# PEER layer in two passes: a larger top-k budget per expert row in the first, leftover blocks spread through the second

## The chip, the cores and the metric

The kernel runs on one core of a Trainium2 chip, as one launch. The metric is the device time of one execution in microseconds (us). The kernel before has a median of 4171.94 us over three runs.

## What is computed

The reference is a float32 model on 256 tokens of width 1024 and 256 context tokens: two blocks of one kind, then two of another. Only the first kind's PEER layer matters here. It is a feed-forward layer that picks experts by product keys:

```python
def chunk(hc):                                   # 128 tokens
    q = (hc @ w_query).reshape(128, 8, 2, 64)
    s = einsum('chpd,hpnd->chpn', q, sub_keys)   # scores of 2 x 128 keys per head
    s_top, i_top = lax.top_k(s, 16)
    cand = s_top[:, :, 0, :, None] + s_top[:, :, 1, None, :]
    best, pos = lax.top_k(cand.reshape(128, 8, 256), 16)
    eid = ...                                    # expert = 128 * i + j, of 16384
    gate = softmax(best)
    act = gelu(einsum('chkd,cd->chk', u_tab[eid], hc)) * gate
    return einsum('chk,chkd->cd', act, v_tab[eid])
```

In the first of the two layers it runs over 512 tokens (x and context), in the second over 256.

## The kernel before

The kernel does not gather experts for most tokens. It computes the activation of all 16384 experts for all tokens, multiplies by a gate matrix that is zero except at each token's picks, and multiplies by the whole V table. All products are made three times in a split of float32 into a high and a low half (`mm3`: high x high, high x low, low x high, lines 371 to 373). Each weight piece is 128 x 1024 (512 KB): it is loaded on the SP queue (`raw`, line 344), rounded to its high half `wh` on ScalarE (line 339), and its low half `wl` is the difference, on VectorE, or on GpSimd for every `share`-th piece (line 340). There are four `raw` buffers and two each of `wh` and `wl`.

`peer(0)` treats the 512 tokens in four groups of 128. The first group (`g0` = 128) is done by rows: its top-k gives expert numbers, `rows_up` gathers one U row per token and step with GpSimd and makes the dot product on VectorE (line 1159), and `rows_down` gathers V rows and accumulates on VectorE (line 1178). The other 384 tokens go through the whole table, in two passes:

- **The U pass.** An expert row is 128 experts: 24 matmuls of 384 columns into one bank, and a gelu on ScalarE (line 1238). A block, `ublock`, is four rows, and there are 32 blocks. After each row the loop takes steps of the top-k generator, `budget` units' worth (each step yields its cost), at a raised priority. It also takes `rate["up"]` steps of `rows_up` once the first group's top-k is ready. The top-k is scores on TensorE, searches on VectorE (lines 1006 to 1061), and for the three table groups a one-hot expansion (lines 1101 to 1133): VectorE writes `oa` and `ob`, TensorE multiplies them, ScalarE copies, GpSimd adds into `stg`, and the gate matrix is stored to `gd` in DRAM. A finished block's activations `a4` are stored to `ad` in DRAM on ScalarE's queue. The pass ends after the block in which the top-k runs out; `nb` is the number of blocks done. A tail follows, in which what remains of the top-k is worked off.
- **The V pass.** The 32 blocks are taken two at a time (`deep` = 2). `prep(b)` loads the block's gates and activations, multiplies them (line 1297) and splits them. For a block that the U pass left over (`b >= nb`) it computes the four expert rows on the spot, with all low halves on VectorE (`share` = 0). Then, for each of eight output slices `d`, 24 matmuls go into one bank and VectorE adds the result to `xt` (line 1304). After each slice come `rate["down"]` steps of `rows_down`. Blocks are prepared up to two ahead. There are two `a4` buffers.

The code is traced in program order, and a planner with its own costs then sets each engine's order from priorities and from what is ready; the engines run their lists strictly in that order. The order of the V blocks is one leftover block first, then all the others by number:

```python
order = list(range(32))
if nb < 32:
    order = [nb] + order[:nb] + order[nb + 1 :]
```

`peer(1)` uses the same function with 256 tokens, no rows and a budget of 2.0. It leaves four blocks to its V pass, one at the start and three at the end.

Of the kernel before, what the change touches and what calls it, by code (L numbers as in the profile page):

```python
# [233 lines left out]
class Kernel:  # L234
# [748 lines left out]
    ratio2 = (1.0, 1.3)  # L983
    on_pool = 6
    pool_x = (0, 0, 0, 0, 0, 0, 0, 0)
    rate = {("gate", 0): (10, 0, 2), ("gate", 1): (4, 0, 2), ("u", 0): 0, ("u", 1): 0, ("v", 0): 0, ("v", 1): 1.25, "mix": (5, 1.3), "up": 1.22, "down": 1.15, "ffn": 1.4, "out": 1, "att": (0.4, 0.4), "norm": ((4,4), (2,2), (4,4), (4,4))}


    def topk(self, l, tt, tp, qT, gd, keep):
# [191 lines left out]
    def peer(self, l, budget):  # L1181
# [3 lines left out]
        g0 = self.rows_at(l)  # L1185
# [4 lines left out]
        with ExitStack() as es:  # L1190
# [7 lines left out]
            up = None  # L1198
# [6 lines left out]
            with self.pool(f"tp{l}") as tp:  # L1205
# [43 lines left out]
                nb = owed = 0  # L1249
                while not done and nb < 32:  # L1250
                    for a4 in ublock(4 * nb):
# [9 lines left out]
                        if g0 and "ready" in dst:  # L1261
                            if up is None:
                                up = self.rows_up(tp, dst, x)
# [17 lines left out]
            with self.pool(f"vp{l}") as vp:  # L1281
# [54 lines left out]
                if g0:  # L1336
                    acc = self.t(vp, [P, D], "racc")
                    down = self.rows_down(vp, dst, acc)
                    self.steps = 0
                order = list(range(32))  # L1340
                if nb < 32:
                    order = [nb] + order[:nb] + order[nb + 1 :]
                todo = [prep(b) for b in order[: wb - deep]]
                bias = self.bias_load(vp) if l == 0 else None
# [312 lines left out]
    def run(self):  # L1657
        self.setup()

        self.filler = self.adaln(self.mod1[0], self.v("b_mod0"))  # L1660
        for s in (1, 0):
            cols = slice(s * T, s * T + T)
            self.nc.sync.dma_start(self.xt[:, :, cols], self.A["xt"][:, :, cols])
            for d in range(8):
                self.track(d, s)
        self.mixer(0)
        self.need(60)
        if self.stop == "mix0":
            return self.dump()

        self.peer(0, 3.1)
        if self.stop == "peer0":
            return self.dump()
        self.mixer(1)
        if self.stop == "mix1":
            return self.dump()
        self.peer(1, 2.0)
        if self.stop == "peer1":
            return self.dump()
        with self.more_weights(2, 0), self.pool("bp") as bp:  # L1680
            self.bp = bp
            with self.banks(sc=2):
                self.enter(0, 0)
            self.sums_begin(bp, 2, (2,), self.sums_of("adat", 72, self.mod2[1], "ada_b1", lambda m: (2,)))
            self.ffn(0, 0, (0, 1))
            self.mixer2(0, (0, 2))
            self.ffn(0, 1, (1, 0))
            self.ffn(1, 0, (1, 1))
            self.mixer2(1, (1, 2))
            self.ffn(1, 1, None)  # L1690
# [20 lines left out]
```

## Time and profile before

| | |
|---|---|
| median of 3 runs | 4171.94 us (4168.49 to 4172.41) |
| the profiled execution | 4176.94 us, span 4175.2 us |
| TensorE busy, mean granted clock | 92% of the span, 0.945 |
| VectorE busy | 77% |
| ScalarE, GpSimd busy | 43%, 23% |
| DMA | 944.96 MB, mean 226 GB/s |

The time is that of the whole execution, and the span runs from the first to the last instruction in the trace. Busy is the share in which an engine executes. A granted clock of 1.00 is TensorE's full speed. PEld is TensorE's weight load, which overlaps its matmuls.

### The profile page before, as it was taken

Reading aid. Unit: us, or ns where it says so; the run is one execution under the profiler, and the core shown is the slowest. Engines: PE = TensorE matmul, PEld = TensorE weight load, DVE = VectorE, ACT = ScalarE, POOL = GpSimd, SP = SyncE. Lnnn points to the kernel's source line nnn. Section 1 sums busy time; section 2 is a strip of 40 time slices with the busy share of each in tenths; the row PEclk is TensorE's granted clock in tenths of the full one; section 3 lists DMA queues with packets and bytes.
Section 4 is the critical chain, followed back from the end, with each engine's and each line's share of the span. In section 5 each row is a group of like instructions: output and inputs, shape, how many; then the busy total and the mean of one; then the engine's idle time right before and its main releaser. Section 6 shows DMA issues by size and latency. Waiting matters only on the chain.

```text
span 4175.2 us, 69284 instructions
## 1 busy us (share of the span) xinstructions
PE 3820.4 (92%) x25443; PEld 3562.4 (85%) x25443; DVE 3235.8 (77%) x7950; ACT 1794.7 (43%) x2986; POOL 968.9 (23%) x803
## 2 busy tenths in 40 slices
PE   7889898978897699999899999999989989999898
PEld 5568798978786599998689999999989879998798
DVE  4768778988987699996768997898868778656664
ACT  3342333433444233333344656444444554444543
POOL 0100014654634233440302848000000010100100
PEclk9999999999896799999899999999999989999899
DMA  5436548888756999984235767999869439554244
GB/s 181 157 103 216 184 156 292 290 287 279 251 191 176 254 348 345 340 324 140 98 117 186 251 234 254 378 363 341 310 232 315 155 104 320 159 184 146 95 162 142
DMA packets 331123, 944.96 MB, mean 226 GB/s; under 512 B 30832, under 2 KB 118512, under 8 KB 330784
## 3 DMA queue, kind: packets, MB, share of 16 engines
q1 hardware_dynamic: 201776, 722.15, 49.8%
q0 software_dynamic: 38272, 137.38, 10.3%
q10 hardware_dynamic: 90736, 81.01, 5.9%
q8 instruction: 201, 3.29, 0.3%
q14 instruction: 138, 1.13, 0.1%
HBM read 855.23 MB, written 85.19 MB: 225 GB/s over the span
## 4 chain that ended last, share of the span: by engine, by line
PE 46%; DVE 8%; issue 7%; DMA 3%; ACT 1%; POOL 1%; another core or an unknown queue 1%; ACTq 0%; SPq 0%; DVEq 0%; POOLq 0%
PE mm L373 14%; PE mm L371 14%; PE mm L372 14%; DVE wl L340 2%; DMA raw<-in_vt 2%; DVE cj L1061 1%; ACT wh L339 1%; PE sc L1122 1%; DMA arow<-in_adat 1%; DMA gd<-stg 1%; DVE cacc L770 1%; DVE w4l L340 0%; DVE nu L535 0%; PE sc L510 0%
## 5 line engine op out<-in xcount | busy, mean ns | idle before, releaser
L339 ACT ACTIVATE wh<-raw 128x1024 fp32r<-128x1024 f32 x946 | 997.0, 1057 | 1535.0 <-PE mm L372 1173.3
L340 DVE TENSOR_TENSOR wl<-raw,wh 128x1024 fp32r<-128x1024 f32 x840 | 1054.6, 1259 | 446.4 <-ACT wh L339 439.2
L373 PE MATMUL mm<-h2h,wl 128*128 128x256 f32 (+2 forms) x2176 | 694.5, 320 | 61.6 <-DVE wl L340 57.2
L371 PE MATMUL mm<-h2h,wh 128*128 128x256 f32 (+2 forms) x2176 | 692.7, 320 | 20.7 <-ACT a L1238 13.8
L372 PE MATMUL mm<-h2l,wh 128*128 128x256 f32 (+2 forms) x2176 | 692.2, 318 | 0.0
L371 PE MATMUL mm<-w4h,wh 128*128 128x384 f32 (+1 forms) x2048 | 631.8, 312 | 26.0 <-ACT wh L339 25.8
L373 PE MATMUL mm<-w4h,wl 128*128 128x384 f32 (+1 forms) x2048 | 601.2, 312 | 35.2 <-DVE wl L340 35.1
L372 PE MATMUL mm<-w4l,wh 128*128 128x384 f32 (+1 forms) x2048 | 630.3, 311 | 2.3 <-DVE w4l L340 2.3
L371 PE MATMUL mm<-h,wh 128*128 128x256 f32 x1712 | 498.4, 291 | 16.5 <-ACT h L540 6.7
L372 PE MATMUL mm<-h,wh 128*128 128x256 f32 x1712 | 494.4, 289 | 2.4 <-DVE h L541 1.8
L373 PE MATMUL mm<-h,wl 128*128 128x256 f32 x1712 | 490.7, 287 | 0.5 <-DVE wl L340 0.5
L373 PEld LDWEIGHTS mm<-h2h,wl 128*128 128x128 f32 x2176 | 425.4, 196 | 74.1 <-DVE wl L340 65.3
L371 PEld LDWEIGHTS mm<-h2h,wh 128*128 128x128 f32 x2176 | 425.4, 196 | 27.8 <-ACT a L1238 16.6
L372 PEld LDWEIGHTS mm<-h2l,wh 128*128 128x128 f32 x2176 | 425.4, 196 | 2.7
L373 PEld LDWEIGHTS mm<-w4h,wl 128*128 128x128 f32 x2048 | 383.3, 191 | 42.1 <-DVE wl L340 41.8
L371 PEld LDWEIGHTS mm<-w4h,wh 128*128 128x128 f32 x2048 | 391.3, 192 | 31.2 <-ACT wh L339 30.2
L372 PEld LDWEIGHTS mm<-w4l,wh 128*128 128x128 f32 x2048 | 391.5, 191 | 2.8 <-DVE w4l L340 2.8
L371 PEld LDWEIGHTS mm<-h,wh 128*128 128x128 f32 x1712 | 335.5, 196 | 24.2 <-ACT h L540 10.4
L372 PEld LDWEIGHTS mm<-h,wh 128*128 128x128 f32 x1712 | 335.2, 196 | 9.7 <-DVE h L541 7.1
L340 POOL TENSOR_TENSOR wl<-raw,wh 128x1024 fp32r<-128x1024 f32 x106 | 260.2, 2455 | 345.2 <-ACT wh L339 332.1
L373 PEld LDWEIGHTS mm<-h,wl 128*128 128x128 f32 x1712 | 334.9, 196 | 0.7 <-DVE wl L340 0.7
L1146 POOL DMA_INDIRECT vr<-in_vg,rowid x128 | 196.0, 1531 | 375.3 <-DVE racc L1178 350.6
(356 smaller groups left out, 7413.0 us busy)
## 6 DMA issues: line engine op xcount, KB each, us to landing
raw<-in_ut SPq DMA_DIRECT2D x256, 512.0 KB
raw<-in_vt SPq DMA_DIRECT2D x256, 512.0 KB
raw<-in_wgu SPq DMA_DIRECT2D x176, 512.0 KB
arow<-in_adat SPq DMA_DIRECT2D x144, 512.0 KB
raw<-in_wdn SPq DMA_DIRECT2D x88, 512.0 KB
gd<-stg ACTq DMA_DIRECT2D x20, 2048.0 KB
raw<-in_win SPq DMA_DIRECT2D x66, 512.0 KB
raw<-in_wmod SPq DMA_DIRECT2D x48, 512.0 KB
```

What stands on the lines that cost most here:

```text
L339: self.nc.scalar.activation(h, src, AF.Copy)
L340: (eng or self.nc.vector).tensor_sub(l, src, h.bitcast(F32))
L371: mm(out, wh, xh, start=start, stop=False)
L372: mm(out, wh, xl, start=False, stop=False)
L373: mm(out, wl, xh, start=False, stop=stop)
L770: nc.vector.scalar_tensor_tensor(av[:, cc], u[:, cc, :, k : k + T], w[:, cc * 31 + k : cc * 31 + k + 1], av[:, cc], op0=OP.mult, op1=OP.add,)
L1061: nc.vector.scalar_tensor_tensor(junk, self.iota[:, :NCAND], pf[:, h, k : k + 1], eid[:, h, :], op0=OP.is_equal, op1=OP.mult, accum_out=se ...
L1122: nc.tensor.matmul(pg[:, j * 256 : (j + 1) * 256], oa[:, 2 * h + j], obs[h][:, j].rearrange("p a b -> p (a b)"), start=True, stop=True,)
L1146: self.nc.gpsimd.indirect_dma_start(out=r, out_offset=None, in_=self.A[table], in_offset=bass.IndirectOffsetOnAxis(ap=ids[:, i : i + 1], a ...
```

## The change

Three edits, all in layer 0's PEER. The U pass takes 3.9 units of the top-k per expert row instead of 3.1; `rows_up` takes 1.65 steps per row instead of 1.22; and where the layer has a row group (`g0`, layer 0 alone), the leftover blocks are no longer first and last in the V pass but spread between the others in even steps.

```diff
-    rate = {("gate", 0): (10, 0, 2), ("gate", 1): (4, 0, 2), ("u", 0): 0, ("u", 1): 0, ("v", 0): 0, ("v", 1): 1.25, "mix": (5, 1.3), "up": 1.22, "down": 1.15, "ffn": 1.4, "out": 1, "att": (0.4, 0.4), "norm": ((4,4), (2,2), (4,4), (4,4))}
+    rate = {("gate", 0): (10, 0, 2), ("gate", 1): (4, 0, 2), ("u", 0): 0, ("u", 1): 0, ("v", 0): 0, ("v", 1): 1.25, "mix": (5, 1.3), "up": 1.65, "down": 1.15, "ffn": 1.4, "out": 1, "att": (0.4, 0.4), "norm": ((4,4), (2,2), (4,4), (4,4))}
...
                 order = list(range(32))
-                if nb < 32:
+                if g0:
+                    order.sort(key=lambda b: ((b - nb) / (32 - nb), 0) if b >= nb else (b / nb, 1))
+                elif nb < 32:
                     order = [nb] + order[:nb] + order[nb + 1 :]
...
-        self.peer(0, 3.1)
+        self.peer(0, 3.9)
```

## Rows read from the trace of the kernel before

**Rows 1.** Page: engine totals of the whole span; granted clock in 40 slices

```profile
PE 3820.4 (92%) x25443; PEld 3562.4 (85%) x25443; DVE 3235.8 (77%) x7950; ACT 1794.7 (43%) x2986; POOL 968.9 (23%) x803
...
PEclk9999999999896799999899999999999989999899
```

**Rows 2.** Busy time of four stretches (first line names the columns)

```profile
core 0: us, PE busy (x) PEld busy (x) DVE busy (x) ACT busy (x) POOL busy (x), PEclk, DMA share, GB/s
555.00:1318.00 763.00, 661.20 (x3437) 625.06 (x3437) 680.52 (x2624) 304.86 (x477) 381.87 (x361) 0.90 0.72 244
...
1243.00:1318.00 75.00, 57.36 (x153) 41.42 (x154) 68.14 (x155) 39.32 (x67) 47.68 (x64) 0.54 0.43 130
1318.00:1420.00 102.00, 55.12 (x255) 51.37 (x254) 41.27 (x68) 21.66 (x37) 16.87 (x12) 0.75 0.98 227
1420.00:1937.00 517.00, 508.07 (x2900) 500.85 (x2898) 476.30 (x725) 178.21 (x244) 181.55 (x120) 1.00 0.89 321
```

**Rows 3.** Lines of the U pass, 555 to 1318 us, all engines

```profile
L1159 DVE SCALAR_TENSOR_TENSOR ur<-ur,xg 128x1024 f32<-128x1024 f32 x128 | 154.2, 1211 | 30.5 <-DMA ur<-in_ug,rowid 30.3
...
L340 DVE TENSOR_TENSOR wl<-raw,wh 128x1024 fp32r<-128x1024 f32 x84 | 122.5, 1458 | 19.9 <-ACT wh L339 15.8 <-PE sc L1122 3.7
...
L340 POOL TENSOR_TENSOR wl<-raw,wh 128x1024 fp32r<-128x1024 f32 x41 | 98.5, 2402 | 171.1 <-ACT wh L339 160.3 <-PE sc L1122 6.5 <-PE mm L373 3.9
```

**Rows 4.** Waits of VectorE in the U pass: total us, times, longest

```profile
DVE ur L1159 <- DMA ur<-in_ug,rowid: 30.3, 15, 6.4
DVE top L1006 <- ACT s L1001: 16.9, 3, 10.5
DVE wl L340 <- ACT wh L339: 15.8, 15, 2.9
```

**Rows 5.** Timeline of TensorE at the end of the tail

```profile
1310.11 1.66 PE L1122 MATMUL sc<-ob,oa 128*128 128x256 f32 x4 [0.50 <-DVE ob L1111]
1311.57 0.53 PE L371 MATMUL mm<-h2h,wh 128*128 128x384 f32 x1
```

**Rows 6.** Timeline of VectorE over the same end

```profile
1309.49 1.65 DVE L1111 SCALAR_TENSOR_TENSOR ob<-io,top,ix 128x256 fp32r<-128x256 f32 x4
1318.39 1.22 DVE L340 TENSOR_TENSOR wl<-raw,wh 128x1024 fp32r<-128x1024 f32 x1 [7.25 <-ACT wh L339]
```

**Rows 7.** Busy time of the V pass in its steady part

```profile
1420.00:1900.00 480.00, 471.28 (x2686) 464.41 (x2685) 451.65 (x677) 164.26 (x221) 181.55 (x120) 1.00 0.93 337
```

**Rows 8.** Waits of TensorE in the V pass

```profile
PE mm L373 <- DVE wl L340: 5.6, 10, 1.4
PE mm L371 <- ACT wh L339: 3.1, 11, 0.3
```

**Rows 9.** Waits of the SP queue in the V pass

```profile
SPq L344 <- DVE wl L340: 302.9, 115, 6.3
SPq L1293 <- DVE w4l L340: 74.7, 26, 4.2
```

**Rows 10.** Timeline of TensorE inside one expert row of the U pass

```profile
1182.95 0.33 PE L371 MATMUL mm<-h2h,wh 128*128 128x384 f32 x1
...
1183.99 0.33 PE L371 MATMUL mm<-h2h,wh 128*128 128x384 f32 x1
```

**Rows 11.** Timeline of ScalarE: expert rows inside layer 1's V pass

```profile
2925.82 0.38 ACT L1238 ACTIVATE a<-mm 128x256 f32<-128x256 f32 x1 [4.58 <-PE mm L373]
...
2954.62 0.38 ACT L1238 ACTIVATE a<-mm 128x256 f32<-128x256 f32 x1 [0.94 <-PE mm L373]
```

**Rows 12.** Waits of TensorE at the start of the V pass

```profile
PE mm L373 <- DVE wl L340: 23.4, 2, 12.3
```

**Rows 13.** DMA issues: KB each

```profile
raw<-in_ut SPq DMA_DIRECT2D x256, 512.0 KB
...
ad<-a ACTq DMA_DIRECT2D x31, 768.0 KB
a<-ad SPq DMA_DIRECT2D x31, 768.0 KB
```

## Prediction

> **What bounds the kernel now.** I read the page first, to see which engine fills the span. TensorE is busy 92% and VectorE 77%, but these are averages, and the granted clock falls to 0.6 and 0.7 only in the 13th and 14th of the 40 slices, 1253 to 1461 us [rows 1]. There the first PEER layer's U pass ends and its V pass begins, so I split that layer into stretches [rows 2]. The reader should see two stages with different limits.
>
> The U pass takes 763 us, from 555 us to 1318 us. VectorE works 680.5 us of it, because it carries the top-k, the expert rows' dot products (L1159, 154.2 us) and two thirds of the weight splits [rows 2, 3]. TensorE is the waiting party. Its expert rows are all done at 1243 us, and for the next 75 us it makes only the last one-hot products, at a granted clock of 0.54, most of the time the lower of its two levels, 1.2 GHz, while VectorE is busy 68.1 of the 75 [rows 2]. So in this stage the time is VectorE's work plus VectorE's own idle time, 763 - 680.5 = 82.5 us. The list of its waits gives the larger parts: 30.3 us for gathered rows, 16.9 us for the next top-k's scores, 15.8 us for ScalarE's high halves [rows 4].
>
> The V pass is the opposite. After a start of 102 us with DMA at 0.98 it runs at full clock, with TensorE busy 508.1 of 517 us [rows 2], and the list of TensorE's waits finds 5.6 + 3.1 us in that time [rows 8]. In its steady part 2686 matmuls take 480 us, 0.179 us each [rows 7]. Inside a single expert row of the U pass, where nothing waits, six matmuls of the same width start within 1183.99 - 1182.95 = 1.04 us, 0.173 us each [rows 10]. The V pass therefore runs within 3% of TensorE's own pace.
>
> **What the change moves.** The top-k generator yields 1.0 + 16 x 1.1 + 4.0 + 8 x 0.7 + 32 x 0.75 = 52.2 units for the first 128 tokens and 2.0 + 32 x 1.7 = 56.4 more for each of the other three groups: 4 x 52.2 + 3 x 56.4 = 378.0. Each expert row adds 3.1 or 3.9 units, so it is used up in row 122 or row 97 (378 / 3.1 = 121.9, 378 / 3.9 = 96.9). The block under way is finished, so the U pass has 31 blocks before, as the 31 stores of `ad` confirm [rows 13], and 25 after. Six blocks, 24 expert rows of 24 matmuls, go from the U pass to the V pass. Nothing is removed from TensorE's work.
>
> **Price in the V pass.** A row costs 24 x 0.173 = 4.16 us at the U pass's pace, 24 x 0.179 = 4.29 us at the V pass's. That is 100 to 103 us for 24 rows, and I take 101. There is no idle TensorE time in the steady V pass to hide it in. The nearest case is in layer 1, where the last leftover blocks already run inside the V pass: eleven results, ten rows, stand 2954.62 - 2925.82 = 28.8 us apart, 2.88 us for 24 narrower matmuls [rows 11]. Rows there pay their full price. The low end lets one block (17 us) fall into the start of the V pass, where TensorE waits 23.4 us for low halves alone [rows 12]: 84 us.
>
> The moved rows' other instructions: 24 weight loads of 512 KB on SP, 24 high halves and 24 gelus on ScalarE (busy 178 of 517 us), and 24 splits on VectorE at 1.22 us [rows 6], 29 us on an engine with 41 us idle there plus the 101 us of new TensorE time. These lie beside TensorE. If the cover failed, the split would be late next, since TensorE's only sizeable wait is already for it [rows 8]. Six stores and six loads of activations, 768 KB each, go [rows 13]. GpSimd's queue in the V pass holds the row gathers, and nothing that moves joins it. One wait is new: a leftover block holds one of two activation buffers until its four rows are done, and an SP load for a later block waits for it, with weight loads queued behind that and TensorE behind those. The existing waits of that kind are 74.7 us over 26, mean 2.9 us [rows 9], and with them TensorE still waits only 8.7 us [rows 8]; so I take 0, and 6 x 2.9 = 17 us at the high end: 120. Reordering the V blocks changes only which two share a group.
>
> **Gain in the U pass.** VectorE loses the splits of 24 rows. It had 84 of 125, the rest being GpSimd's [rows 3], so 16 splits at 1.22 to 1.46 us, 20 to 23 us. The top-k and the 128 dot products stay; a rate of 1.65 steps per row for 1.22 only makes up for there being fewer rows. GpSimd loses 8 splits of 2.4 us; it is busy half the pass [rows 2] and sets nothing. That leaves 680.5 - 22 = 658 us of work. Idle time is the open term: with fewer rows VectorE waits less for ScalarE and TensorE, but the gathers and the three changes of token group remain. Below I keep the gather and score waits, 47 us, and 8 us more, 55; above, 100, if denser steps wait longer for gathers. I take 75, near the present 82.5. The U pass then takes 733 us (713 to 758): a gain of 30 us (5 to 50).
>
> **The sum.** 101 - 30 = +71 us on the profiled execution's 4176.9 us (its span of 4175.2 and 1.7 us around it): 4248. That execution is 5.0 us above the median of the three runs, so 4243 us against 4171.9. With the bounds, 84 - 50 = +34 to 120 - 5 = +115: 4206 to 4287.
>
> **Rivals.** *The V pass is paced by DMA.* For it: DMA is busy 0.93 at 337 GB/s there [rows 7]. Then rows cost only their bytes: 24 x 0.524 MB of weights less 6 x 0.786 MB of loads, 7.9 MB, 23 us at that rate. The result is 4172 + 23 - 30 = 4165 us. Against it: weight loads on SP wait 302.9 us for a buffer that a split frees, not the other way [rows 9], and TensorE is not starved [rows 8]. It decides if the V pass grows by less than 40 us. The Trainium skill (Perfetto Trace Analysis, Engine Utilization) gives 358 GB/s as a core's memory peak and so puts this stretch at 94% of it; by that rule the 7.9 MB would be the price, 22 us. The trace agrees that the rate is high, but not that TensorE waits for it.
>
> *The planner pulls leftover rows into the stretches where TensorE idles.* They need nothing of the top-k. The tail's 153 matmuls would fill some 25 us of 75 at full pace, and the V start's 255 some 45 us of 102 [rows 2], so 24 rows would fit. All hidden, the result is 4172 - 30 = 4142 us, faster; faster by 0.2% needs 19 of the 24 rows hidden. Against it: block 31 was free to run in the tail before, yet its matmuls start at 1311.57 us, right behind the last one-hot product [rows 5], and its next split stands behind VectorE's last top-k work [rows 6].
>
> *TensorE's clock falls in the U pass.* After the change it has 100 rows x 4.16 us, plus 384 one-hot products of 256 columns, which at layer 1's 2.88 / 24 = 0.12 us [rows 11] are 46 us: 462 us in 733. Below a granted share of 462 / 733 = 0.63 it would become the limit; at 0.60 the stage takes 770 us, 37 us more, and the run 4280 us. The tail's 0.54 speaks for it, the whole pass's 0.90 against it [rows 2]. The Trainium skill (TensorE: Matmul & The Clock Gate, Part 1) says that the throttled clock is the default and activity lifts it, which the 0.54 of the tail agrees with; taken over the whole pass it would give that higher time.
>
> **Chances.** My forecast holds 0.76. The low clock has 0.07, DMA pacing 0.09, hoisted rows 0.08. About 0.2%, 8 us, is what a measurement of this kernel can tell from no change. DMA pacing gives 7 us less, on that edge: half same, half faster. So faster 0.12, same 0.05, slower 0.83. For 8 in 10 the range reaches a little past the forecast's own 4206 to 4287 us on the low side, where a partial hoist would fall: 4195 to 4287.
>
> **What would show it.** Right: 25 stores of `ad`; a U pass of 713 to 758 us with VectorE over 0.87 busy; a tail, between the last expert row's result and the next block's first, of at least 75 us; a V pass about 100 us longer, TensorE still over 0.96 busy. Wrong: a V pass less than 40 us longer, leftover matmuls among the last one-hot products, a U pass shorter by 70 us or more, or an unchanged number of blocks.

## The result, and the profile after

The changed kernel takes 4214.73 us (median of three runs, 4213.61 to 4217.11) against 4171.94 us. The ratio is 1.0106, with a 95% interval of 1.0083 to 1.0129: 1% slower. The forecast was 4243 us, 4195 to 4287, slower with 0.83.

The page's engine totals and the granted clock by slice, to be read beside [rows 1]:

```profile
PE 3806.7 (90%) x25443; PEld 3551.6 (84%) x25443; DVE 3239.6 (77%) x7958; ACT 1795.9 (43%) x2986; POOL 940.9 (22%) x795
...
PEclk9999999999857999999999999999999989999999
```

TensorE's busy share falls from 92% to 90%. The dip of the clock now lies in the 12th and 13th slices.

Busy time of four stretches of the changed kernel, cut at the same events as in [rows 2] (from 4.5 us before the first expert row's result to 6.2 us after the last one-hot product; inside it the tail, from the last expert row's result; the next 102 us; the V pass to its last matmul):

```profile
556.00:1262.00 706.00, 558.43 (x2861) 521.48 (x2860) 653.79 (x2608) 269.38 (x428) 365.06 (x353) 0.87 0.71 239
1127.00:1262.00 135.00, 63.99 (x173) 45.94 (x172) 124.11 (x636) 44.81 (x77) 48.71 (x66) 0.54 0.31 94
1262.00:1364.00 102.00, 55.63 (x271) 51.45 (x270) 43.76 (x72) 24.10 (x39) 16.97 (x12) 0.78 0.98 228
1364.00:1976.00 612.00, 603.36 (x3460) 598.45 (x3459) 505.79 (x744) 213.13 (x290) 170.81 (x120) 1.00 0.80 284
```

Set beside [rows 2], the U pass goes from 763 to 706 us, the start of the V pass keeps its 102 us, and the rest of the V pass goes from 517 to 612 us. So 57 us are won in the first stage and 95 us lost in the second; what lies before and behind them is 1.4 us shorter in all, so the two spans differ by 36.6 us. The limits are as before: VectorE is busy 653.8 of the U pass's 706 us, TensorE 603.4 of the V pass's 612 us.

VectorE's longest waits inside the U pass (561 to 1256 us), beside [rows 4], and the lines of its splits, beside [rows 3]:

```profile
DVE ur L1159 <- DMA ur<-in_ug,rowid: 25.1, 25, 3.9
DVE wl L340 <- ACT wh L339: 9.5, 6, 3.4
DVE top L1006 <- ACT s L1001: 6.4, 2, 4.0
```

```profile
L340 DVE TENSOR_TENSOR wl<-raw,wh 128x1024 fp32r<-128x1024 f32 x67 | 95.8, 1430 | 9.6 <-ACT wh L339 9.5
L340 POOL TENSOR_TENSOR wl<-raw,wh 128x1024 fp32r<-128x1024 f32 x33 | 79.3, 2403 | 109.0 <-ACT wh L339 107.4 <-PE sc L1122 1.3
```

The wait for the next token group's scores falls from 16.9 to 6.4 us, the wait for ScalarE's high halves from 15.8 to 9.5 us, the wait for gathered rows from 30.3 to 25.1 us. VectorE makes 67 splits instead of 84, and they take 95.8 us instead of 122.5.

TensorE at the end of the tail, beside [rows 5]:

```profile
1254.08 1.67 PE L1122 MATMUL sc<-ob,oa 128*128 128x256 f32 x4 [0.50 <-DVE ob L1111]
1255.54 0.52 PE L371 MATMUL mm<-h2h,wh 128*128 128x384 f32 x1
```

The leftover block again starts directly behind the last one-hot product. None of its matmuls, nor of the six blocks after it, runs inside the tail, where TensorE has little to do for 129 us.

A leftover block inside the V pass, by ScalarE's results for its four rows:

```profile
1486.04 0.47 ACT L1238 ACTIVATE a<-mm 128x384 f32<-128x384 f32 x1
...
1490.20 0.47 ACT L1238 ACTIVATE a<-mm 128x384 f32<-128x384 f32 x1
...
1494.54 0.47 ACT L1238 ACTIVATE a<-mm 128x384 f32<-128x384 f32 x1
...
1498.52 0.47 ACT L1238 ACTIVATE a<-mm 128x384 f32<-128x384 f32 x1
```

Three steps take 12.48 us, 4.16 us each, just the pace of [rows 10]. TensorE's waits in the V pass (1364 to 1976 us), beside [rows 8], and at its start (1262 to 1364 us), beside [rows 12]:

```profile
PE mm L373 <- DVE wl L340: 7.1, 9, 1.3
PE mm L371 <- ACT wh L339: 1.4, 5, 0.3
```

```profile
PE mm L373 <- DVE wl L340: 23.3, 3, 13.6
PE mm L371 <- ACT wh L339: 21.6, 3, 16.0
```

Nothing new appears in either list. The wait that the prediction called new, for an activation buffer, stands in the list of the SP queue, beside [rows 9]; it is smaller than before (29.2 us against 74.7):

```profile
SPq L1293 <- DVE w4l L340: 29.2, 15, 3.4
```

The DMA issues, beside [rows 13], confirm 25 blocks:

```profile
raw<-in_ut SPq DMA_DIRECT2D x256, 512.0 KB, 4.6
...
ad<-a ACTq DMA_DIRECT2D x25, 768.0 KB, 5.6
a<-ad SPq DMA_DIRECT2D x25, 768.0 KB, 7.1
```

### The profile page after: what moved, and what is told of

Read it like the earlier page. It is cut to its first block, busy times and chain, and to the rows that moved or that the text cites. A ratio compares the mean times of both kernels' runs of the same rounds, so it can differ in the third digit from the quotient of the medians.

```text
span 4211.8 us, 69206 instructions
## 1 busy us (share of the span) xinstructions
PE 3806.7 (90%) x25443; PEld 3551.6 (84%) x25443; DVE 3239.6 (77%) x7958; ACT 1795.9 (43%) x2986; POOL 940.9 (22%) x795
## 4 chain that ended last, share of the span: by engine, by line
PE 45%; DVE 9%; issue 7%; DMA 5%; ACT 1%; POOL 1%; another core or an unknown queue 0%; ACTq 0%; SPq 0%; DVEq 0%; POOLq 0%
PE mm L373 14%; PE mm L371 14%; PE mm L372 14%; DVE wl L340 2%; DMA a<-ad 2%; DMA raw<-in_vt 1%; DVE cj L1061 1%; ACT wh L339 1%; PE sc L1122 1%; DVE a L1297 1%; DMA arow<-in_adat 1%; DMA gd<-stg 1%; DVE w4l L340 1%; DVE cacc L770 0%
## 5 line engine op out<-in xcount | busy, mean ns | idle before, releaser
L340 DVE TENSOR_TENSOR wl<-raw,wh 128x1024 fp32r<-128x1024 f32 (+1 forms) x848 | 1057.0, 1249 | 481.8 <-ACT wh L339 479.3
L340 POOL TENSOR_TENSOR wl<-raw,wh 128x1024 fp32r<-128x1024 f32 x98 | 241.0, 2459 | 285.0 <-ACT wh L339 280.9
L1129 POOL TENSOR_TENSOR stg<-s 128x256 f32<-128x256 f32 x320 | 265.5, 852 | 148.1 <-ACT s L1127 86.7
```

What stands on the lines that cost most here:

```text
L340: (eng or self.nc.vector).tensor_sub(l, src, h.bitcast(F32))
L1129: nc.gpsimd.tensor_tensor(stg[:, :, c : c + 2].rearrange("p b t -> p t b"), both[:, :, 0], both[:, :, 1], op=OP.add)
```

## The experiments

Two stage times are compared throughout, each from one profiled execution and rounded to 1 us. The U pass is counted from the first expert row's result to the last one-hot product, the V pass from its first to its last matmul. The 18 us between them are the same within 1 us in most runs. The time behind the V pass, which no edit touches, lies between 2230 and 2242 us in these profiles, so a stage says more than a span. Each ratio is to runs of the kernel before that were taken beside the kernel's own; their medians were 4164.57 to 4171.94 us. The U and V pass of the kernel before, and the U pass of the changed kernel:

```profile
560.00:1312.00 752.00, 650.20 (x3382) 614.11 (x3381) 678.99 (x2620) 300.83 (x473) 378.92 (x360) 0.90 0.72 245
1330.00:1937.00 607.00, 551.20 (x3084) 540.22 (x3082) 511.52 (x782) 194.70 (x271) 193.77 (x128) 0.96 0.90 306
```

```profile
561.00:1256.00 695.00, 547.43 (x2807) 510.53 (x2806) 652.15 (x2604) 265.55 (x425) 362.28 (x352) 0.87 0.71 241
```

A single profile is uncertain. Three kernels here whose edits leave the U pass alone (the changed one, the old order, the one without V rows) show 695, 696 and 690 us, and two that leave the V pass alone (the changed one and the one without dot products) 702 and 707 us, so differences of some 6 us say nothing. A profiled execution can also differ from its kernel's other runs: that of the kernel before took 5 to 12 us more than the medians of its runs, that of "budget 3.9 alone" 7 us less than its median. Where a stage and a ratio differ, the ratio decides.

| kernel | expert rows in the U pass | U pass | VectorE busy | VectorE idle | V pass | ratio to the kernel before (95%) |
|---|---|---|---|---|---|---|
| before | 124 | 752 | 679 | 73 | 607 | 1 |
| changed | 100 | 695 | 652 | 43 | 702 | 1.0106 (1.0083 to 1.0129) |
| old order of V blocks | 100 | 696 | 655 | 41 | 701 | 1.0106 (1.0083 to 1.0130) |
| old rate 1.22 | 100 | 701 | 657 | 44 | 709 | 1.0125 (1.0097 to 1.0153) |
| budget 3.5, rate 1.45 | 112 | 705 | 659 | 46 | 656 | 1.0003 (0.9985 to 1.0022) |
| budget 3.9 alone, 31 blocks | 124 | 714 | 671 | 43 | 609 | 0.9949 (0.9924 to 0.9973) |
| budget 3.9, rate 1.65, 31 blocks | 124 | 725 | 672 | 53 | 604 | 0.9945 (0.9926 to 0.9964) |
| the same, added splits on GpSimd | 124 | 727 | 660 | 67 | 606 | 0.9928 (0.9905 to 0.9952) |
| the same, every second split on GpSimd | 124 | 731 | 660 | 71 | 603 | 0.9957 (0.9936 to 0.9979) |
| the same, all 32 blocks | 128 | 732 | 674 | 58 | 613 | 0.9991 (0.9976 to 1.0007) |
| rate 1.65 alone | 124 | 735 | 673 | 62 | 605 | 0.9963 (0.9949 to 0.9977) |
| rate 2.2 alone | 124 | 733 | 672 | 61 | 604 | 0.9953 (0.9930 to 0.9976) |

**What paces each pass.** Two kernels take work out of the changed one; each ran once. The first has no dot products on VectorE in the U pass:

```diff
                 r = todo.pop(0)
-                self.nc.vector.scalar_tensor_tensor(
-                    r, r, 1.0, x, op0=OP.mult, op1=OP.mult, accum_out=dst["dot"][:, i - 2 : i - 1]
-                )
+                if i == 2:
+                    self.nc.vector.tensor_copy(dst["dot"], x[:, 0:P])
+                self.nc.scalar.activation(dst["dot"][:, i - 2 : i - 1], r[:, 0:1], AF.Copy)
```

> Changed kernel that leaves out VectorE's 128 dot products of the row group in the U pass (154 us of VectorE's work); the rows are still gathered, and a short ScalarE copy takes the place of each product, so the row group's gate weights are wrong. Theory (the U pass is paced by VectorE): U pass 695 us shorter by 110 to 170 us, run 4045 to 4105 us. Rival (it is paced by gathers, by TensorE or by the order of steps): shorter by less than 50 us.

It took 4100.17 us. Its U pass by the view of stretches:

```profile
560.00:1129.00 569.00, 515.28 (x2809) 492.11 (x2808) 510.10 (x2348) 278.68 (x554) 364.80 (x352) 0.93 0.84 294
```

VectorE's work falls by 142 us (652 to 510) and the stage by 126 us (695 to 569), with the same 128 gathers and 100 rows. The U pass follows VectorE.

The second gathers one V row per token and no more:

```diff
-        todo = []
-        for i in range(P + 3):
...
+        r = self.fetch(pool, "vr", 4, "vg", dst["id"], 0)
+        self.nc.vector.tensor_scalar(acc, r, dst["dot"][:, 0:1], None, op0=OP.mult)
+        yield
```

> Changed kernel that gathers and accumulates one V row per token instead of 128 (it leaves out 127 gathers of 512 KB, 67 MB, and 162 us of VectorE's work in the V pass). Theory (the V pass is paced by TensorE): matmul pace falls at most from 0.178 to 0.173 us, 17 us over the pass, and the start of the V pass may lose up to 40 us of waits; run 4155 to 4205 us. Rival (the V pass is paced by DMA, which loses over a third of its bytes): V pass shorter by 100 us or more, run below 4115 us.

It took 4195.55 us. The whole V pass, first of the changed kernel, then of this one:

```profile
1274.00:1976.00 702.00, 646.98 (x3659) 637.91 (x3658) 543.47 (x804) 230.60 (x318) 183.02 (x128) 0.97 0.83 275
```

```profile
1272.00:1959.00 687.00, 642.45 (x3663) 637.75 (x3661) 401.37 (x678) 231.26 (x318) 2.42 (x4) 0.97 0.60 185
```

DMA falls from 275 to 185 GB/s and VectorE's work from 543 to 401 us, and the pass is shorter by 15 us of 702. So neither DMA nor VectorE sets the pace of the V pass; TensorE, busy 603 of its last 612 us, does. The Trainium skill (Perfetto Trace Analysis, Engine Utilization) gives 358 GB/s as a core's memory peak, and adds that this is the share of a core whose partner uses the memory too, and that a core alone can pull more. The kernel before ran this pass at up to 94% of that figure [rows 7], the changed one at 275 GB/s on average, 77%. This run shows that the figure did not set the pace of the changed kernel; no run here takes bytes away from the kernel before.

**The order of the V blocks.**

```diff
-                if g0:
-                    order.sort(key=lambda b: ((b - nb) / (32 - nb), 0) if b >= nb else (b / nb, 1))
-                elif nb < 32:
+                if nb < 32:
```

> Changed kernel with the old order of V blocks: one leftover block first, six at the end. Theory (each pass has its own limit: a row costs TensorE's time wherever it stands in the V pass): V pass within 8 us of the changed kernel's 702 us, run 4207 to 4223 us. Rival (the even spreading hides part of the rows beside the DMA load): the six blocks packed at the end cost 10 to 25 us more, 4225 to 4240 us. Rival (spreading itself costs something): below 4205 us.

4209.01 us, the same ratio as the changed kernel, with a V pass of 701 us. Spreading the leftover blocks neither costs nor hides anything. That fits a TensorE that waits only 8.5 us in the last 612 us of the pass.

**The rate.** In the changed kernel back to 1.22, then in the kernel before raised to 1.65, then to 2.2 (here and below, only the entry that changes is shown of a long line):

```diff
-"up": 1.65
+"up": 1.22
...
-"up": 1.22
+"up": 1.65
...
-"up": 1.22
+"up": 2.2
```

> Changed kernel with the old rate of 1.22 dot-product steps per expert row; 23 or so of the 128 steps are then left for the end of the U pass. Theory (the U pass is VectorE's work plus its idle time, and the work is the same): U pass 690 to 715 us against 695, run 4205 to 4235 us, the upper half only if the late steps wait for their gathers. Rival (the higher rate is what took VectorE's idle time from 82 to 53 us): VectorE idle back to 75 us or more, run 4235 us or more.

4218.69 us: within the theory's range; VectorE's idle time stays at 44 us.

> Kernel before with the rate of 1.65 steps alone, budget 3.1 and 31 blocks as before. Theory: VectorE's work is the same, so the U pass stays within 10 us of 752 us and the run between 4162 and 4182 us. Rival (the rate is what saves idle time): U pass 20 to 30 us shorter, run 4140 to 4152 us.

4152.08 us, and 0.37% faster than the kernel before. The theory failed here. The U pass, 17 us shorter:

```profile
560.00:1295.00 735.00, 647.41 (x3386) 611.23 (x3385) 672.73 (x2620) 302.58 (x474) 379.64 (x359) 0.91 0.74 251
```

Of the 17 us, 11 are idle time and 6 are VectorE's work: the same 83 splits take less time each (1.46 us before, 1.37 here). Where the top-k is handed out at 3.1, the rate does shorten the U pass.

> Kernel before with 2.2 dot-product steps per row alone, budget 3.1. If an earlier end of the row group keeps taking idle time away: U pass 715 to 728 us against 735 at 1.65, run 4130 to 4145 us. If the effect was spent at 1.65 or came from one place in the planner's order: 730 to 750 us, run 4148 to 4170 us.

4148.99 us, U pass 733 us: spent at 1.65.

**The number of rows.**

```diff
-        self.peer(0, 3.9)
+        self.peer(0, 3.5)
...
-"up": 1.65
+"up": 1.45
```

> Changed kernel with budget 3.5 and 1.45 steps: 28 blocks in the U pass, 12 rows moved instead of 24. Theory (a moved row costs 4.0 us in the V pass and gives 2.4 us back in the U pass): +19 us on the kernel before, 4184 to 4200 us, with the V pass at 655 us and the U pass at 724 us. Rival (the gain in the U pass comes from where the groups of tokens change over, not from the number of rows): no straight line; at or below 4175 us, or at 4210 us.

4171.87 us, as fast as the kernel before and below the 4175 us of the rival. The theory failed: it had the V pass right (656 us) and the U pass 19 us too long (724 against 705). No straight line runs through the kernel before: half the rows give 47 of the 57 us of the U pass's gain (752 to 705) and only half of the V pass's loss (49 of 95 us). So something else in the U pass had been won that does not depend on the rows. The next two runs look for it: they keep budget 3.9 and rate 1.65 and go on to 31 blocks; only the first of them has the last two lines, which give every split of the added rows to GpSimd.

```diff
-                while not done and nb < 32:
+                while not (done and nb >= (31 if g0 else 0)) and nb < 32:
+                    if done:
+                        self.share = 1
```

> Changed kernel whose U pass goes on to 31 blocks after the top-k has been handed out at 3.9 units per row; the low halves of the 24 added rows are all made by GpSimd, one block stays for the V pass. Theory (the loss is that rows were taken out of the stage where TensorE waits and set into the one where it does not): V pass back to 607 us, U pass 695 to 725 us, run 4115 to 4148 us, faster than both. Rival (the rows cost their time in either place, because they stand behind the top-k): U pass grows by 80 to 100 us, run 4195 to 4215 us.

4142.39 us, 0.72% faster than the kernel before and within the expected range; the U pass, at 727 us, is 2 us above its own.

> As the run above, but with the low halves of the added rows two thirds on VectorE and one third on GpSimd, as in the kernel before: the larger budget and rate alone, with 31 blocks. Theory: U pass 20 to 25 us longer than in the changed kernel for 16 more splits on VectorE, 715 to 735 us, V pass 607 us, run 4135 to 4160 us. Rival (rows behind the top-k starve): 4195 to 4215 us. Rival (fewer rows is what saves VectorE's idle time): U pass 745 us or more, run 4165 us or more.

4148.05 us, 0.55% faster, as the theory said. With the 24 rows back, the U pass grows by 30 us (695 to 725) and the V pass shrinks by 98 us (702 to 604). The rows no longer wait behind the whole top-k: traced after its last step, they run beside the fourth group's searches and one-hot products. ScalarE's last result of a row comes 44 us before the end of the last one-hot product here, 128 us before it in the changed kernel:

```profile
1239.11 0.47 ACT L1238 ACTIVATE a<-mm 128x384 f32<-128x384 f32 x1
```

```profile
1282.07 1.67 PE L1122 MATMUL sc<-ob,oa 128*128 128x256 f32 x4 [0.50 <-DVE ob L1111]
```

The same with the old rate:

```diff
-"up": 1.65
+"up": 1.22
```

> Budget 3.9 with the old rate of 1.22, 31 blocks in the U pass as before. It splits the 28 us that the U pass gained with both and with 31 blocks (752 to 725 us), of which the rate alone gave 17 (735 us). If each edit takes idle time of its own: U pass 738 to 746 us, run 4150 to 4160 us. If the denser top-k does all of it and the rate is one way among several to break up the same waits: U pass 720 to 732 us, run 4137 to 4150 us. If only the rate counts: U pass 748 us or more, run 4162 us or more.

4141.31 us, 0.51% faster, with a U pass of 714 us, a little below what was expected if the denser top-k does all of it. This kernel and the one with the old rate and 25 blocks are the cleanest pair: same budget, same rate, 24 rows here or there. U and V pass of each, first with 25 blocks, then with 31:

```profile
560.00:1261.00 701.00, 551.79 (x2807) 514.14 (x2806) 656.64 (x2604) 265.77 (x424) 351.85 (x352) 0.86 0.70 239
1278.00:1987.00 709.00, 649.96 (x3663) 640.74 (x3661) 545.03 (x806) 231.41 (x321) 184.38 (x128) 0.96 0.82 273
```

```profile
561.00:1275.00 714.00, 629.64 (x3384) 597.91 (x3383) 671.39 (x2620) 299.23 (x473) 384.05 (x359) 0.93 0.76 259
1293.00:1902.00 609.00, 551.24 (x3087) 539.44 (x3085) 512.04 (x783) 195.19 (x272) 184.84 (x128) 0.96 0.89 305
```

In these profiles the rows are worth 13 us in the U pass and cost 100 us in the V pass, 4.2 us each. The budget alone, at 31 blocks, takes the U pass from 752 to 714 us, 30 of the 38 us from VectorE's idle time. Both figures lean on one quick execution of the kernel with 31 blocks and one long one of the kernel before: by the ratio, the budget alone is worth 21 us of the whole run, not 38. The rate adds nothing to that (0.9945 with it, 0.9949 without).

**Two attempts to go further.** Every second split on GpSimd, and all 32 blocks in the U pass, each on the kernel with budget 3.9, rate 1.65 and 31 blocks:

```diff
-    shares = (3, 2)
+    shares = (2, 2)
...
-nb >= (31 if g0 else 0)
+nb >= (32 if g0 else 0)
```

> Budget 3.9, rate 1.65, 31 blocks, and every second low half of the whole U pass on GpSimd instead of every third, 20 fewer on VectorE. If the U pass is VectorE's work plus an idle time that stays at 53 us: work 672 less 25, U pass 697 to 705 us, run 4115 to 4130 us. If GpSimd's halves, at 2.4 us each, give idle time back as in the run with GpSimd alone for the added rows (53 to 67 us): U pass 710 to 728 us, run 4130 to 4150 us.

4149.63 us, at the upper end of the second expectation, with a U pass of 731 us, 3 us above it. VectorE loses 12 us of work and gains 18 us of idle time. In the lists of waits, first without, then with the extra splits on GpSimd, its wait for TensorE to free one-hot operands grows:

```profile
DVE ob L1111 <- PE sc L1122: 5.2, 8, 1.2
```

```profile
DVE ob L1111 <- PE sc L1122: 25.2, 21, 5.1
```

> Budget 3.9, rate 1.65, all 32 blocks in the U pass and none left over. Between the last one-hot product and the first V matmul lie 18 us in every run so far, and the one leftover block runs in them. If those 18 us are set by the gate matrix's way through DRAM: they stay, empty of TensorE work, the V pass stays at 604 us, the U pass grows by up to 8 us, run 4146 to 4158 us. If they are set by the leftover block itself: 18 us shorter, less what the U pass grows, run 4132 to 4142 us.

4161.23 us, 3 us above the first expectation. TensorE between the last one-hot product and the first V matmul, and VectorE's first instruction on the gates:

```profile
1296.64 1.67 PE L1122 MATMUL sc<-ob,oa 128*128 128x256 f32 x4 [0.50 <-DVE ob L1111]
1319.39 1.01 PE L371 MATMUL mm<-w4h,wh 128*128 128x384 f32 x2 [21.08 <-ACT w4h L339]
```

```profile
1318.22 1.96 DVE L1297 TENSOR_TENSOR a<-a,g 128x384 f32<-128x384 f32 x4 [20.40 <-DMA g<-gd]
```

The gap stays, 21 us instead of 18, now empty, and VectorE waits through it for the gates from DRAM. The one leftover block of the kernel before ran in time that stays empty without it. The U pass is 7 us longer, as expected; the V pass is 9 us longer (604 to 613), which was not expected and whose cause stays open.

## Why the prediction was right, and where it was off

**Direction and mechanism: right.** The U pass is VectorE's and the V pass TensorE's, shown by the two runs without work. Moving rows from the one to the other is a loss, shown by the two pairs that differ in the rows alone. The order of the blocks changes nothing.

**Price in the V pass: right.** 101 us forecast, 95 us measured between the kernels (607 to 702), 98 and 100 us in the two pairs that differ in the rows alone. The rows cost 4.16 us each where they stand. The waits at the start, 23.3 and 21.6 us, are no shorter than the 23.4 us of [rows 12], so no block was hidden there. The new wait for an activation buffer cost nothing: SP's waits of that kind came to 29.2 us, and TensorE waits 8.5 us in all after the start.

**Gain in the U pass: mis-sized.** I took 30 us, at most 50; it was 57, and the U pass of 706 us lies below the 713 to 758 us that I had named as a sign of being right. The work term was close: 22 us forecast, 27 measured, of which the fewer splits are the whole (122.5 to 95.8 us). The step that failed is the idle term: I took 75 us, near the present 82.5, and 55 at the least; counted in the same stretch it was 52 us (706 less 653.8; 43 us in the narrower stage of the table). One sentence led there: that the waits for gathers and at the changes of token group remain. Of the 47 us that I kept for them, 31.5 were left: gathers fell from 30.3 to 25.1 us and scores from 16.9 to 6.4. The other candidate, that the rate "only makes up for there being fewer rows", did little harm: with the old rate the changed kernel has 44 us idle too. It is false only at budget 3.1.

The runs showed that the idle time depends on how densely the planner is given VectorE work: with 124 rows and every third split on GpSimd it is 73 us at budget 3.1, 61 to 62 with the rate alone, 43 to 53 with the larger budget. More splits on GpSimd bring it back to 67 and 71. What the denser work gives, 27 to 38 us of the stage in these profiles, has nothing to do with moving rows. The rows alone are worth 13 to 30 us there by the profiles. By the ratios the two pairs differ by 67 and 74 us, each uncertain by 12 to 16; less the 98 and 100 us of the V pass, that leaves some 26 to 31 us for the rows. Within that uncertainty this agrees with the 30 us of the forecast; what I missed is the part that comes from the density.

So the change is two things under one number. The denser top-k gains about 0.5%, and taking six blocks out of the U pass, which the same number brings about, loses 1.6 to 1.8% (1.0106 against 0.9945, 1.0125 against 0.9949). Why denser work leaves fewer gaps was not isolated; only the waits that shrink are seen, in the changed kernel the one for the next group's scores most of all. It stays open which places in the planner's order account for it.

**The rivals.** DMA pacing is refuted (the V pass grew by 95 us, not under 40, and a third fewer bytes shortened it by 15 of 702 us). The low clock did not come: the U pass was granted 0.87. Hoisted rows did not come either with the change as written, but rows do run beside the end of the top-k once they are issued in the U pass. The tail was forecast at 75 us or more and is 137 us up to the next block's first result. One figure for it was too high: of the 153 matmuls in the old tail 124 are one-hot products, and at 0.12 us for each of those and 0.173 for the rest they would fill 20 us, not 25, which changes nothing.

**A faster kernel.** Budget 3.9 with 31 blocks beats both kernels in each of its four forms, at ratios from 0.9928 to 0.9957. The rate alone, with no other change to the kernel before, gives 0.9963 and 0.9953. The intervals overlap, so the runs do not say which of these is fastest.

## What to carry to other kernels

Ask of each stage which engine it waits for, before moving work between stages: work that is cheap where an engine idles costs its full time where that engine is the limit. When one constant sets two things, here how densely a chain is issued and when a loop ends, change them one at a time. And an engine's idle time in a planned order is a term of its own: it needs bounds of its own, since a new order can shrink it, and not the value of the kernel before.

## What the runs showed of the hardware that was not expected

A split by GpSimd takes 2.40 us and one by VectorE 1.22 us in the V pass, where GpSimd splits nothing, but 1.35 to 1.52 us on average in the U pass of the kernels of the table; taking 12 us of splits off VectorE there shortened nothing. The matmul pace in the V pass varies a little: from 1380 us on, 3360 matmuls in 596 us are 0.177 us each in the changed kernel, and without the V rows 3324 in 579 us are 0.174 us.
